# Weight sums by accumulating transfers, a fifth pair of weight buffers and another product order in a seven-product multiplication

## The chip, the cores and the metric

The kernel runs on one core of a Trainium2 chip. TensorE (PE) multiplies, VectorE (DVE) and ScalarE (ACT) do the elementwise work, GpSimd (POOL) does a little of it and issues the transfers that add to their destination, and SyncE (SP) issues most of the others. The metric is the device time of one execution in microseconds (us); lower is better.

## The reference

Two layers act on h, 512 tokens by 2048 channels. Layer 0 holds an attention and a recurrent mixer; the change does not touch it. Layer 1 is a gated unit with a spatial mix, and a second projection that gates a per-layer embedding:

```python
xn = rms_norm(h, norm_pre[1])
u, v, g = split(xn @ c_w_in, (2048, 2048, 2048))
u, v = gelu(u), layer_norm(gelu(v), c_ln_g, c_ln_b)
mixed = einsum('gts,nsgc->ntgc', tril(c_w_s), v in 4 chunks of 128 tokens and 16 groups) + c_b_s
y = ((u * mixed) * silu(g)) @ c_w_out
h = h + rms_norm(y, norm_post[1])
out = h + (p[1] @ ple_w_proj[1]) * sigmoid(h @ ple_w_gate[1])
```

All arrays are float32, and the weights come from HBM.

## The kernel before

**Numbers.** A float32 operand is split in a high part (a cast by ScalarE) and a low part (the rest, a subtraction by VectorE). A product of two operands is three matmuls: high by high, high by low, low by high. The parts of W are made in `pieces`: line 1453 casts, line 1454 subtracts, for one block of 128 rows by 512 columns at a time. They lie in the tiles `whi` and `wlo`, each with four buffers (pool `wsp`).

**Seven products.** The matrices c_w_in (three of 2048 x 2048, for v, u and g), c_w_out and ple_w_gate[1] are multiplied in `seven` (line 1459), in the manner of Strassen and Winograd. W is handled in pairs: a pair covers 1024 columns, as two column halves of 512 and two row halves of 1024. That gives four blocks, W(row half, column half), and seven products take the place of eight. Each product uses one sum of blocks of W and one sum of blocks of the activations, which was prepared before (`sums`). A product has eight steps, one for each 128 rows; a step is six matmuls of 512 columns in line 1489 (twelve of 256 columns in the multiplication by c_w_out).

The W side of the products, per two rows of blocks (128 x 1024 tiles, index j from 0 to 3):

- 1: W(0,0), loaded by SP (line 1401); the tile is kept as `E[j]`
- 5: `E[j]` plus W(0,1), added by an accumulating transfer that POOL issues (`grow`, line 1405)
- 2: W(1,0), loaded
- 6: W(1,1) is loaded and kept as `H[j]`; VectorE adds it to `E[j]` (line 1409)
- 3: `H[j]`, or W(1,1) loaded afresh if `H` is gone
- 7: `H[j]` plus W(0,1), an accumulating transfer
- 4: `E[j]` plus W(1,0), the last block. A pair with `whole` set uses an accumulating transfer of 512 KB. Any other pair loads two halves of 256 KB (line 1446) and VectorE adds each (line 1409). The halves lie in `half0` and `half1`, one buffer each; the very last pair of the kernel has eight slots of its own (`yl8` to `yl15`).

In the kernel before, `whole` is set for both pairs of g and for the first pair of the last matrix. v, u, c_w_out and the second pair of the last matrix load halves.

**Order.** c_w_in goes v, u and g in turn: the two pairs of v interleaved (`FIRST`), then u's first pair, g's first, u's second, g's second, each in the order 1, 2, 5, 6, 3, 4, 7 (`NEXT`). c_w_out and ple_w_gate[1] use `FIRST` too; its last pair ends with 5, 6 and then 3, 4, 7, or what the caller names: 4, 7, 3 in the last matrix. What is done with finished products (lines 1494 to 1538) writes sums to `comb` tiles and emits results: for the last matrix a sigmoid (line 1275), a multiplication with a fetched tile `pj` (1276), an addition (1278) and a store (1280).

**Beside it.** A clock counts steps (`tick`), and `later` hangs other work on it. During u and g that is the mix, 16 groups: a load of v's rows from HBM (`sq` from `vd`, line 1594, issued by ScalarE), four normalizations by ScalarE (1603), POOL masking the mix weights (1606), two VectorE operations (1607, 1608), the split in parts (1613 to 1619), three matmuls (1624 to 1626) and a product into u (1628). The group number e of each half starts 38 + int(7.1 e) steps after u's second product, its load 11 steps sooner, its normalization 4 sooner. In the last matrix `first_fetch` brings `pj` tiles; those of n = 1 lie in `half0` and `half1`.

Each engine's order of instructions is fixed when the program is built: by program order, by priorities (the casts and subtractions of W have a raised one) and by when an operand and a buffer are expected to be there.

Of the kernel before, what the change touches and what calls it, by code (L numbers as in the profile page):

```python
# [9 lines left out]
F32 = mybir.dt.float32  # L10
F32R = mybir.dt.float32r
AF = mybir.ActivationFunctionType
ALU = mybir.AluOpType
# [3 lines left out]
P = 128  # L17
T = 512
# [51 lines left out]
def f(ap):  # L70
# [3 lines left out]
FIRST = lambda a, b, end=(3, 4, 7): [  # L74
    (b, 1, False), (a, 1, True), (b, 2, True), (a, 2, True),
    *[(a, n, True) for n in (5, 6, 3, 4, 7)], *[(b, n, True) for n in (*NEXT[2:4], *end)],
]
# [18 lines left out]
class Pair:  # L96


    def __init__(self, W, c0, n, emit):
        self.W, self.c0, self.n, self.emit = W, c0, n, emit  # L100
        self.whole, self.half = False, None
        self.E, self.H, self.acc, self.R, self.done = {}, {}, {}, {}, set()


class Net:
# [911 lines left out]
    def run(self):  # L1017
        tc = self.tc
        with ExitStack() as ctx:
            pool = lambda name, bufs: ctx.enter_context(tc.tile_pool(name=name, bufs=bufs))  # L1020
            cp, xp = pool("cp", 1), pool("xp", 1)
            self.wraw, self.wsp = pool("wraw", 2), pool("wsp", 4)
            self.xp = xp
            dp = ctx.enter_context(tc.tile_pool(name="dp", bufs=1, space=bass.MemoryType.DRAM))
            self.yd = [self.t(dp, [P, T], f"yd{n}") for n in range(8)]
            self.gd = [self.t(dp, [P, T], f"gd{n}") for n in range(len(AHEAD))]
            self.fd = self.t(dp, [16, T], "fd")
            self.xd = self.t(dp, [P, KT, T], "xd")
            self.hd = self.t(dp, [P, KT, T], "hd")
            self.pd = self.t(dp, [P, 4, D], "pd")  # L1030
            self.vd, self.yd2 = (self.t(dp, [P, c, 4, P], n) for n, c in (("vd", KT), ("yd2", 8)))
            self.homes = {}
            self.clock, self.todo = 0, []
            self.ahead = {}
            self.weng = tc.nc.vector
            self.side, self.beats, self.gate_ins = [], 0, (None, None)
            self.y = [None] * 16
            self.layer_ab(cp, pool)
            self.rest(cp)
# [83 lines left out]
    def last_layer(self, cp, fs, turn, wp, ps):  # L1123
        nc, tc, i = self.nc, self.tc, self.i
# [4 lines left out]
        accq = [self.t(wp, [P, T], "accq", bufs=1), self.rstdB]  # L1129
# [74 lines left out]
        nxt, _, x2, s1, s24, s3, x22 = self.sums(H, wp, SETS)  # L1204
# [36 lines left out]
        def fetch(n, m, o):  # L1241
            pj[n, m] = o
            nc.sync.dma_start(o, self.pd[:, m, n * T : (n + 1) * T])

        def first_fetch(n):
            for m in range(2):
                fetch(n, m, self.t(self.wq, [P, T], f"half{m}") if n == 1 else self.slot("yh", 2 - n + m, F32))

        def next_fetch():
            for j, ns in enumerate(((1, 0), (3, 2))):  # L1250
# [31 lines left out]

        W = i["ple_w_gate"][1]
        pairs = [Pair(W, 2 * j * T, 2 * j, emit) for j in range(2)]
        pairs[0].whole = True
        pairs[1].half = lambda k: self.slot("yl", 8 + k, F32)
        self.seven(FIRST(*pairs, (4, 7, 3)), Sets(nxt), ps)
        self.clock += 100
        self.tick()

# [99 lines left out]
    def pieces(self, pr, prod, keep):  # L1390


        nc = self.nc
        block = lambda kh, ch, j: pr.W[
            (8 * kh + 2 * j) * P : (8 * kh + 2 * j + 2) * P, pr.c0 + ch * T : pr.c0 + ch * T + T
        ].rearrange("(k p) c -> p k c", p=P)
        view = lambda tl: tl.rearrange("p (k c) -> p k c", c=T)

        def load(*where):
            tl = self.piece()  # L1400
            nc.sync.dma_start(view(tl), block(*where))
            return tl

        def grow(tl, *where):
            nc.gpsimd.dma_start(view(tl), block(*where), accum_op=ALU.add)

        def add(tl, other):
            with self.tc.high_priority(self.wpri):
                nc.vector.tensor_tensor(tl, tl, other, ALU.add)

        for j in range(4):
            done = None
            if prod == 1:
                tl = load(0, 0, j)
                if keep:
                    pr.E[j] = tl
                else:
                    done = tl
            elif prod == 5:
                if j not in pr.E:  # L1420
                    pr.E[j] = load(0, 0, j)
                tl = pr.E[j]
                grow(tl, 0, 1, j)
            elif prod == 2:
                tl = done = load(1, 0, j)
            elif prod == 6:
                pr.H[j] = load(1, 1, j)
                tl = pr.E[j]
                add(tl, pr.H[j])
            elif prod == 3:  # L1430
                if j in pr.H:
                    tl = pr.H[j]
                else:
                    tl = done = load(1, 1, j)
            elif prod == 7:
                tl = done = pr.H.pop(j)
                grow(tl, 0, 1, j)
            elif pr.whole:
                tl = done = pr.E.pop(j)
                grow(tl, 1, 0, j)  # L1440
            else:
                tl = done = pr.E.pop(j)
                for a in range(2):
                    g = pr.half(2 * j + a) if pr.half else self.t(self.wq, [P, T], f"half{a}")
                    k = 8 + 2 * j + a
                    nc.sync.dma_start(g, pr.W[k * P : (k + 1) * P, pr.c0 : pr.c0 + T])
                    add(tl[:, a * T : (a + 1) * T], g)
            for a in range(2):
                src = tl[:, a * T : (a + 1) * T]
                hi = self.t(self.wsp, [P, 512], "whi", F32R)  # L1450
                lo = self.t(self.wsp, [P, 512], "wlo", F32R)
                with self.tc.high_priority(self.wpri):
                    self.cast = nc.scalar.copy(hi, src)  # L1453
                    nc.vector.tensor_tensor(lo, src, f(hi), ALU.subtract)  # L1454
                yield 2 * j + a, hi, lo
            if done is not None:
                self.gone(done)

    def seven(self, order, sets, ps, after=lambda n: None, fm=False):


        nc, tc = self.nc, self.tc
        for step, (pr, prod, keep) in enumerate(order):
# [3 lines left out]
            acc = pr.acc[{2: 1, 3: 5}.get(prod, prod)]  # L1467
# [5 lines left out]
            for k, hi, lo in self.pieces(pr, prod, keep):  # L1473
                rows.append((k, hi, lo))
                if k not in hold:
                    for m in range(2):
                        for r, hi, lo in rows:
                            xh, xl = hs[r // 2][:, r % 2, :], ls[r // 2][:, r % 2, :]
                            more = dict(skip_group_check=True)
                            for a in range(2) if fm else (None,):  # L1480
# [7 lines left out]
                                for j, (x, y) in enumerate(parts):  # L1488
                                    nc.tensor.matmul(  # L1489
                                        o, x, y, start=(first and r == 0 and j == 0 and not a), stop=(r == 7 and j == 2), **more  # L1490
# [3 lines left out]
            for m in range(2):  # L1494
                a = acc[m]
# [12 lines left out]
                        nc.vector.scalar_tensor_tensor(a, a, -1.0, pr.R[1][:, m], ALU.mult, ALU.subtract)  # L1508
                        pr.emit(pr, m, pr.n + 1, a)
            pr.done.add(prod)  # L1510
            if prod == 4 and 7 not in pr.done:
                if 3 not in pr.done:
                    for m in range(2):
                        c22, u = pr.R[5][:, m], pr.R[1][:, m]
                        nc.vector.tensor_tensor(c22, c22, u, ALU.add)
                        nc.vector.tensor_tensor(acc[m], acc[m], u, ALU.subtract)
            elif prod == 7 and 3 not in pr.done:
                for m in range(2):
                    c22 = pr.R[5][:, m]
                    nc.vector.tensor_tensor(c22, acc[m], c22, ALU.add)  # L1520
                    pr.emit(pr, 2 + m, pr.n + 1, c22)
                c21 = self.t(self.rp, [P, 2, T], "comb")
                for m in range(2):
                    nc.scalar.copy(c21[:, m], acc[m])
                    nc.vector.tensor_tensor(c21[:, m], pr.acc[4][m], c21[:, m], ALU.subtract)
                    pr.emit(pr, 2 + m, pr.n, c21[:, m])
            elif prod == 7:
                u3 = pr.R[7] = pr.R[1]
                for m in range(2):
                    nc.vector.tensor_tensor(u3[:, m], acc[m], pr.R[1][:, m], ALU.add)  # L1530
                    c22 = pr.R[5][:, m]
                    nc.vector.tensor_tensor(c22, c22, u3[:, m], ALU.add)
                    pr.emit(pr, 2 + m, pr.n + 1, c22)
                if 4 in pr.done:
                    for m in range(2):
                        u = u3[:, m]
                        nc.vector.tensor_tensor(u, pr.acc[4][m], u, ALU.subtract)
                        pr.emit(pr, 2 + m, pr.n, u)
            after(step)

    def add_sq(self, accq, src, n, wp):
# [11 lines left out]
    def layer_c(self, cp, sets, accq, after, wp, ps):  # L1553
# [79 lines left out]
        V = [Pair(W, D + 2 * j * T, 2 * j, vals) for j in range(2)]  # L1633
        U = [Pair(W, 2 * j * T, 2 * j, gates) for j in range(2)]
        G = [Pair(W, 2 * D + 2 * j * T, 2 * j, silu) for j in range(2)]
        for pr in G:
            pr.whole = True
        order = FIRST(*V)
        for pr in (U[0], G[0], U[1], G[1]):
            order += [(pr, prod, True) for prod in NEXT]  # L1640
# [30 lines left out]
        def done(step):  # L1671
# [20 lines left out]
            for j in range(2):  # L1692
                if step == nv + 14 * j + 1:
                    for e in range(8):
                        mix(8 * j + e, 38 + int(7.1 * e))
            if step == nv + 13:
                for n in range(2):
                    self.later(4, lambda n=n: saved(n))
# [290 lines left out]
```

## Time and profile before

| | us |
|---|---|
| three runs, median | 2249.3 |
| lowest and highest | 2247.73, 2253.25 |
| the profiled execution, whole | 2247.82 |
| its span in the profile | 2245.8 |
| granted TensorE clock, mean | 0.997 |
| c_w_in: first product starts at | 1385.9 |
| u's first pair starts at | 1540.0 |
| multiplication by c_w_out starts at | 1882.7 |
| last matrix starts at | 2074.5 |
| last matmul starts at | 2238.5 |

The times come from a profiler record of one execution. Its page gives busy time by engine, a strip of 40 slices, DMA queues, the chain that ended last and the costliest groups of instructions. Further views give who waited for whom, the busy time of chosen stretches, and instructions in order of time. "PE busy" counts each matmul from its start to its modelled end; neighbouring matmuls overlap, so it can show a busy engine while it loses time. In a group, `whi<-rq` means that a tile `whi` was written from a tile `rq`; W's tiles are called `raw` and `rq`, v's rows are `sq`, accumulators in PSUM are `mm`. `yl`, `yh`, `xl` and `xh` are the places of the activations' parts, and a change of name in line 1489 marks the next product or pair of products.

### The profile page before, as it was taken

To read this page: it belongs to the slowest core of one execution; us is meant where nothing else is said; L and a number is where in the kernel's file an instruction comes from. 1 tells how busy PE (TensorE), PEld (TensorE's weight loads), DVE (VectorE), ACT (ScalarE), POOL (GpSimd) and SP (SyncE) were. 2 spreads that over 40 slices of the span, in tenths; PEclk is the share of its full clock that TensorE was granted. 3 is DMA by queue.
4 is the path that set the end of the run, shared out by engine and by line. 5 is a ranking of instruction groups with operands and counts; after the bars stand their busy time and mean duration, and the time that the engine had idled before them with its cause. 6 is when DMAs were issued, how large, how long until landed. Compare 5 with 4: busy or idle time off the path is not lost. (4 is left out here: it accounts for less than half of the span.)

```text
span 2245.8 us, 40515 instructions
## 1 busy us (share of the span) xinstructions
PE 2209.3 (98%) x15369; PEld 1835.5 (82%) x15369; DVE 1543.0 (69%) x3000; ACT 1274.4 (57%) x2599; POOL 260.4 (12%) x316
## 2 busy tenths in 40 slices
PE   8999999999999999999999999999999999999998
PEld 7878888888888788887888888888778778998886
DVE  8766667666734777883227346987677678888968
ACT  5545545555543677773235445756565567657754
POOL 2000010101000000000010011110121121010020
PEclk9999999999999999999999999999999999999999
DMA  7322322223233633334334345687677786488695
GB/s 236 92 79 61 84 76 79 79 66 86 71 89 101 212 93 105 99 104 143 97 103 158 121 123 142 169 212 207 179 171 204 180 193 169 137 210 259 196 247 156
DMA packets 294641, 313.79 MB, mean 140 GB/s; under 512 B 14973, under 2 KB 190750, under 8 KB 293422
## 3 DMA queue, kind: packets, MB, share of 16 engines
q1 hardware_dynamic: 247534, 249.32, 36.1%
q0 software_dynamic: 25024, 48.24, 12.4%
q10 hardware_dynamic: 21888, 13.64, 2.3%
q8 instruction: 121, 1.98, 0.4%
q14 instruction: 74, 0.61, 0.1%
HBM read 280.45 MB, written 30.70 MB: 139 GB/s over the span
## 5 line engine op out<-in xcount | busy, mean ns | idle before, releaser
L197 DVE TENSOR_TENSOR wlo<-raw,whi 128x512 fp32r<-128x512 f32 x400 | 283.4, 717 | 300.6 <-ACT whi L195 265.5
L195 ACT CAST whi<-raw 128x512 fp32r<-128x512 f32 x400 | 247.2, 619 | 345.2 <-PE mm L212 144.1
L212 PE MATMUL mm<-xl,whi 128*128 128x512 f32 x1056 | 414.6, 393 | 0.0
L211 PE MATMUL mm<-xh,whi 128*128 128x512 f32 x992 | 412.0, 415 | 0.0
L213 PE MATMUL mm<-xh,wlo 128*128 128x512 f32 x992 | 391.9, 395 | 0.0
L1454 DVE TENSOR_TENSOR wlo<-rq,whi 128x512 fp32r<-128x512 f32 x432 | 292.3, 685 | 117.1 <-ACT whi L1453 115.8
L1453 ACT CAST whi<-rq 128x512 fp32r<-128x512 f32 x432 | 264.9, 620 | 186.2 <-PE mm L1489 111.8
L212 PEld LDWEIGHTS mm<-xl,whi 128*128 128x128 f32 x1056 | 199.3, 189 | 32.3
L213 PEld LDWEIGHTS mm<-xh,wlo 128*128 128x128 f32 x992 | 186.4, 188 | 41.3
L211 PEld LDWEIGHTS mm<-xh,whi 128*128 128x128 f32 x992 | 187.1, 189 | 33.2
L1489 PE MATMUL mm<-whi,yh 128*128 128x512 f32 x512 | 163.9, 395 | 5.2 <-ACT whi L1453 5.2
L1489 PE MATMUL mm<-whi,yl 128*128 128x512 f32 x512 | 163.7, 393 | 1.1 <-ACT comb L1500 1.1
L1489 PE MATMUL mm<-whi,xl 128*128 128x512 f32 x512 | 163.3, 392 | 0.4 <-ACT whi L1453 0.4
L1489 PEld LDWEIGHTS mm<-whi,yh 128*128 128x128 f32 x512 | 96.9, 189 | 27.1 <-ACT whi L1453 6.9
L1489 PEld LDWEIGHTS mm<-whi,yl 128*128 128x128 f32 x512 | 96.0, 188 | 21.9 <-ACT comb L1500 2.0
L1489 PEld LDWEIGHTS mm<-whi,xl 128*128 128x128 f32 x512 | 96.1, 188 | 21.3 <-ACT whi L1453 0.8
L1454 DVE TENSOR_TENSOR wlo<-raw,whi 128x512 fp32r<-128x512 f32 x128 | 86.9, 686 | 30.6 <-ACT whi L1453 30.2
L1453 ACT CAST whi<-raw 128x512 fp32r<-128x512 f32 x128 | 78.3, 621 | 47.6 <-PE mm L1489 27.4
L1489 PE MATMUL mm<-wlo,yh 128*128 128x512 f32 x256 | 102.0, 398 | 2.0 <-DVE wlo L1454 1.9
L1489 PE MATMUL mm<-wlo,xl 128*128 128x512 f32 x256 | 100.2, 392 | 2.6 <-DVE wlo L1454 2.6
L1489 PE MATMUL mm<-wlo,yl 128*128 128x512 f32 x256 | 100.2, 391 | 1.2 <-DVE wlo L1454 1.1
L1489 PE MATMUL mm<-whi,xh 128*128 128x512 f32 x256 | 80.8, 391 | 0.0
(527 smaller groups left out, 4658.6 us busy)
## 6 DMA issues: line engine op xcount, KB each, us to landing
raw<-in_ab_w_in_dram SPq DMA_DIRECT2D x128, 512.0 KB, 3.9
rq<-in_c_w_in_dram SPq DMA_DIRECT2D x50, 512.0 KB, 4.9
rq<-in_c_w_in_dram POOLq DMA_DIRECT2D x44, 512.0 KB, 7.8
raw<-in_ple_w_gate_dram SPq DMA_DIRECT2D x42, 512.0 KB, 4.2
raw<-in_ab_w_out_dram SPq DMA_DIRECT2D x32, 512.0 KB, 3.8
raw<-in_c_w_in_dram SPq DMA_DIRECT2D x26, 512.0 KB, 5.5
rq<-in_c_w_out_dram SPq DMA_DIRECT2D x24, 512.0 KB, 11.5
rq<-in_ple_w_gate_dram SPq DMA_DIRECT2D x22, 512.0 KB, 4.7
```

Of the source, the lines that this page charges most:

```text
L195: nc.scalar.copy(hi[:, : m * n], src)
L197: self.weng.tensor_tensor(lo[:, : m * n], src, f(hi[:, : m * n]), ALU.subtract)
L211: nc.tensor.matmul(acc, hi, xhi[k], start=(k == 0), stop=False)
L212: nc.tensor.matmul(acc, hi, xlo[k], start=False, stop=False)
L213: nc.tensor.matmul(acc, lo, xhi[k], start=False, stop=(k == nk - 1))
L1453: self.cast = nc.scalar.copy(hi, src)
L1454: nc.vector.tensor_tensor(lo, src, f(hi), ALU.subtract)
L1489: nc.tensor.matmul(o, x, y, start=(first and r == 0 and j == 0 and not a), stop=(r == 7 and j == 2), **more)
```

## The change

1. `whole` becomes the default and v's two pairs alone clear it. u's two pairs, both pairs of c_w_out and the second pair of the last matrix now add product 4's last block by accumulating transfers.
2. Where a pair is `whole`, every fifth pair of high and low parts goes to `half0` and `half1` in place of `wsp`.
3. The second pair of the last matrix ends with products 7, 4, 3 in place of 4, 7, 3. The code for finished products has one form for both orders now: product 7 takes a fresh `comb` tile if product 3 is still to come, and the sum that needs both 4 and 7 is emitted behind whichever is later.
4. The `pj` tiles of n = 1 lie in `accq` and `rstdB`, since the halves are in use.
5. The mix's groups start 40 + int(6.8 e) steps after u's second product.

```diff
@@ Pair
-        self.whole, self.half = False, None
+        self.whole = True
@@ run
+            self.turns = 0
@@ last_layer
         def first_fetch(n):
+            if n == 1:
+                places = self.t(wp, [P, T], "accq", bufs=1), self.rstdB
+            else:
+                places = [self.slot("yh", 2 - n + m, F32) for m in range(2)]
             for m in range(2):
-                fetch(n, m, self.t(self.wq, [P, T], f"half{m}") if n == 1 else self.slot("yh", 2 - n + m, F32))
+                fetch(n, m, places[m])
...
-        pairs[0].whole = True
-        pairs[1].half = lambda k: self.slot("yl", 8 + k, F32)
-        self.seven(FIRST(*pairs, (4, 7, 3)), Sets(nxt), ps)
+        self.seven(FIRST(*pairs, (7, 4, 3)), Sets(nxt), ps)
@@ pieces
-                    g = pr.half(2 * j + a) if pr.half else self.t(self.wq, [P, T], f"half{a}")
+                    g = self.t(self.wq, [P, T], f"half{a}")
...
-                hi = self.t(self.wsp, [P, 512], "whi", F32R)
-                lo = self.t(self.wsp, [P, 512], "wlo", F32R)
+                self.turns = (self.turns + 1) % 5
+                if self.turns or not pr.whole:
+                    hi = self.t(self.wsp, [P, 512], "whi", F32R)
+                    lo = self.t(self.wsp, [P, 512], "wlo", F32R)
+                else:
+                    hi, lo = (self.t(self.wq, [P, T], f"half{x}", F32R) for x in range(2))
@@ seven, behind a product
-            if prod == 4 and 7 not in pr.done:
-                if 3 not in pr.done:
-                    for m in range(2):
-                        c22, u = pr.R[5][:, m], pr.R[1][:, m]
-                        nc.vector.tensor_tensor(c22, c22, u, ALU.add)
-                        nc.vector.tensor_tensor(acc[m], acc[m], u, ALU.subtract)
-            elif prod == 7 and 3 not in pr.done:
-                for m in range(2):
-                    c22 = pr.R[5][:, m]
-                    nc.vector.tensor_tensor(c22, acc[m], c22, ALU.add)
-                    pr.emit(pr, 2 + m, pr.n + 1, c22)
-                c21 = self.t(self.rp, [P, 2, T], "comb")
-                for m in range(2):
-                    nc.scalar.copy(c21[:, m], acc[m])
-                    nc.vector.tensor_tensor(c21[:, m], pr.acc[4][m], c21[:, m], ALU.subtract)
-                    pr.emit(pr, 2 + m, pr.n, c21[:, m])
-            elif prod == 7:
-                u3 = pr.R[7] = pr.R[1]
+            if prod == 7:
+                u3 = pr.R[7] = pr.R[1] if 3 in pr.done else self.t(self.rp, [P, 2, T], "comb")
                 for m in range(2):
                     nc.vector.tensor_tensor(u3[:, m], acc[m], pr.R[1][:, m], ALU.add)
...
-                if 4 in pr.done:
-                    for m in range(2):
-                        u = u3[:, m]
-                        nc.vector.tensor_tensor(u, pr.acc[4][m], u, ALU.subtract)
-                        pr.emit(pr, 2 + m, pr.n, u)
+            if prod in (4, 7) and {4, 7} <= pr.done:
+                for m in range(2):
+                    u = pr.R[7][:, m]
+                    nc.vector.tensor_tensor(u, pr.acc[4][m], u, ALU.subtract)
+                    pr.emit(pr, 2 + m, pr.n, u)
@@ layer_c
-        for pr in G:
-            pr.whole = True
+        for pr in V:
+            pr.whole = False
...
-                        mix(8 * j + e, 38 + int(7.1 * e))
+                        mix(8 * j + e, 40 + int(6.8 * e))
```

## The prediction

> **What bounds the kernel now.** I read the page, then the matrix line's own waits, then a table of stretches, then the rows of the engine that comes last. Times are us; a row of a timeline is start, duration, instruction, and in brackets the idle time before it with what ended it.
>
> ```profile
> span 2245.8 us, 40515 instructions
> PE 2209.3 (98%) x15369; PEld 1835.5 (82%) x15369; DVE 1543.0 (69%) x3000; ACT 1274.4 (57%) x2599; POOL 260.4 (12%) x316
> L1454 DVE TENSOR_TENSOR wlo<-rq,whi 128x512 fp32r<-128x512 f32 x432 | 292.3, 685 | 117.1 <-ACT whi L1453 115.8
> L1453 ACT CAST whi<-rq 128x512 fp32r<-128x512 f32 x432 | 264.9, 620 | 186.2 <-PE mm L1489 111.8
> ```
>
> TensorE bounds it, and no edit removes a matmul. So the change can only win back time in which TensorE waits, and only in the seven-product multiplications. The waits of line 1489 name what it waits for, the two parts of W:
>
> ```profile
>   DVE wlo L1454: 21.4, 40
>   ACT whi L1453: 13.2, 10
> ```
>
> "Busy" overlaps pipelined matmuls, so I count lost time by stretches between product boundaries instead: length, then line 1489's matmuls in it (two belong to the neighbours), then further columns, with the granted clock as the third last.
>
> ```profile
> core 0: us, PE busy (x) PEld busy (x), PEclk, DMA share, GB/s
> 1572.66:1594.42 21.76, 21.76 (x98) 18.02 (x96) 1.00 0.69 158
> 1594.42:1622.38 27.96, 24.95 (x97) 18.77 (x96) 0.94 0.68 210
> 1763.28:1790.21 26.93, 23.51 (x97) 17.63 (x96) 1.00 0.76 206
> 1966.84:1978.36 11.52, 11.52 (x99) 11.52 (x98) 1.00 0.99 261
> 2013.78:2026.75 12.97, 11.99 (x99) 11.62 (x97) 1.00 0.95 211
> 2179.93:2191.49 11.56, 11.46 (x49) 8.86 (x48) 1.00 1.10 270
> 2191.49:2205.29 13.80, 11.46 (x50) 8.77 (x48) 1.00 0.94 229
> ```
>
> The first row is the undisturbed pace: two products, 96 matmuls, 21.76; 10.88 a product, 1.36 for one of its eight steps. The second row is products 4 and 7 of u's first pair: 6.20 over. The third is the same place in u's second pair: 5.17 over. In the output projection a product takes 11.52; the product at 2013.78 takes 12.97, 1.45 over. In the last matrix the product at 2191.49, number 6 of the last pair, is 13.80 − 10.88 = 2.92 over.
>
> What comes last in u and g is ScalarE, which also carries the spatial mix and stands in its queue for v's rows:
>
> ```profile
> ACT sq L1603 <- DMA sq<-vd: 42.7, 16, 5.3
> 1600.58 0.49 ACT L1603 ACTIVATE sq<-sq,nb,rv 128x128 f32<-128x128 f32 x1 [3.54 <-DMA sq<-vd]
> 1612.78 1.26 ACT L1603 ACTIVATE sq<-sq,nb,rv 128x128 f32<-128x128 f32 x3 [5.06 <-DMA sq<-vd]
> 1769.73 0.49 ACT L1603 ACTIVATE sq<-sq,nb,rv 128x128 f32<-128x128 f32 x1 [3.83 <-DMA sq<-vd]
> 1782.14 1.26 ACT L1603 ACTIVATE sq<-sq,nb,rv 128x128 f32<-128x128 f32 x3 [5.26 <-DMA sq<-vd]
> 1836.10 0.49 ACT L1603 ACTIVATE sq<-sq,nb,rv 128x128 f32<-128x128 f32 x1 [3.27 <-DMA sq<-vd]
> 1854.33 0.88 ACT L1603 ACTIVATE sq<-sq,nb,rv 128x128 f32<-128x128 f32 x2 [4.16 <-DMA sq<-vd]
> ```
>
> While ScalarE stands there no part of W is cast. With four buffers the casts are at most four steps ahead, 5.44; the step being read (1.36), a cast (0.62) and a subtraction (0.69) come off: 2.77 of cover. The six waits shown are the ones above it. The other ten share 42.7 − 25.1 = 17.6, 1.8 each.
>
> **The change, part by part.**
>
> *Additions moved to transfers.* Five pairs lose eight loads of 256 KB on SP and eight VectorE additions each, and get four accumulating transfers of 512 KB from POOL.
>
> ```profile
> L1409 DVE TENSOR_TENSOR rq<-rq,half x40: 672/691/694, 1442.1 to 2018.4; 128x512 f32<-128x512 f32 x40
> L1446 SPq DMA_DIRECT2D half<-in_c_w_in_dram x32: 327/328/468, 1225.0 to 1749.9; - x32
> L1446 SPq DMA_DIRECT2D half<-in_c_w_out_dram x16: 327/334/346, 1752.0 to 2013.3; - x16
> L1446 SPq DMA_DIRECT2D yl<-in_ple_w_gate_dram x8: 328/362/412, 2182.6 to 2191.9; - x8
> L1405 POOL DMA_DIRECT2D rq<-in_c_w_in_dram x44: 1188/1203/1707, 1396.7 to 1852.7; - x44
> q1 hardware_dynamic: 247534, 249.32, 36.1%
> q0 software_dynamic: 25024, 48.24, 12.4%
> ```
>
> v keeps 16 of the 32 loads, so 16 + 16 + 8 = 40 go, with 40 additions: 40 x 0.691 = 27.6 of VectorE. Most of that is not on the path, since VectorE is 69% busy; it counts only where a late addition stands before a subtraction. There are two such places:
>
> ```profile
> 2018.35 0.69 DVE L1409 TENSOR_TENSOR rq<-rq,half 128x512 f32<-128x512 f32 x1 [1.38 <-DMA half<-in_c_w_out_dram]
> 2198.50 0.69 DVE L1409 TENSOR_TENSOR rq<-rq,yl 128x512 f32<-128x512 f32 x1 [1.48 <-DMA yl<-in_ple_w_gate_dram]
> 2199.85 0.50 PE L1489 MATMUL mm<-wlo,xl 128*128 128x512 f32 x1 [2.34 <-DVE wlo L1454]
> ```
>
> At both, an addition for product 4 waits for its load, VectorE works its queue in order, and subtractions that TensorE needs stand behind it. With the additions gone I take back all of 1.45 and 2.92. Bounds: nothing, if an accumulating transfer is as late; all, if not. I take all, because ScalarE and VectorE ask for product 4's data only when they cast it.
>
> On SP 40 issues of 0.33 go, and with them the places where the next block's load stood behind a waiting one. On POOL 20 issues of 1.20 come, 24.1, on an engine that is 12% busy. Queued behind them are product 7's transfers and the mix's masking; both are due one product (10.88) or more later, and four issues take 4.8.
>
> All the accumulating transfers are q0: 92 of 0.524 MB are 48.2 MB. They occupy 0.124 x 2245.8 / 92 = 3.03 of all sixteen DMA engines each. A load of 256 KB costs 0.361 x 2245.8 / 249.32 x 0.262 = 0.85. So 20 x 3.03 − 40 x 0.85 = 26.5 more engine time over the 633 from 1572.66 to 2205.29, 4%. On a load of v's rows, which takes about 7.3 to land (its issue near 1593.3, ended at 1600.58), that is 0.3; times the six critical waits, 1.8, less what the fifth buffer hides. I charge 1.5; bounds 0 and 6.
>
> *The fifth buffer.* One step more ahead: cover 2.77 + 1.36 = 4.13. The four u waits exceed 2.77 by 0.77, 2.29, 1.06 and 2.49, 6.61 together, and exceed 4.13 by 0.93 and 1.13, 2.06. Measured loss there is 6.20 + 5.17, of which the slower clock is (1 − 0.94) x 27.96 = 1.7; the remaining 9.7 is 1.46 times my 6.61, because the four normalizations lie between the casts as well. Gain: 1.46 x (6.61 − 2.06) = 6.6. The two in g exceed 2.77 by 0.50 and 1.39 and 4.13 by 0.03: 1.46 x 1.86 = 2.7. And the 1.7 of slow clock, which follows the 2.1 idle here:
>
> ```profile
> 1614.60 0.50 PE L1489 MATMUL mm<-whi,yh 128*128 128x512 f32 x1 [2.10 <-ACT whi L1453]
> 1615.32 0.67 PE L1489 MATMUL mm<-wlo,yh 128*128 128x512 f32 x1 [0.22 <-DVE wlo L1454]
> ```
>
> I take the slow clock as a consequence of this stall, so that it goes with it. [...]
>
> *The moved mix.* Its first steps come two k-steps later and the spacing is 6.8 instead of 7.1. The same instructions; it may move a wait either way by a step, 1.36. I cost it at nothing and keep ±3.
>
> *Order 7, 4, 3 in the last pair.* No instruction more, nearly. Product 7 must now find its data one product earlier. POOL issues the four transfers here:
>
> ```profile
> 2180.55 1.20 POOL L1405 DMA_DIRECT2D raw<-in_ple_w_gate_dram  x1 [4.55 <-DVE rq L1409]
> 2192.45 1.20 POOL L1405 DMA_DIRECT2D rq<-in_ple_w_gate_dram  x1 [1.14 <-ACT whi L1453]
> DMA to landing us min/median/max: 5.8/8.2/15.0
> ```
>
> Product 7 would begin near 2191.49 + 10.88 = 2202.4; its last block is read six steps later, 2210.5, and cast 1.3 before. 2192.45 + 8.2 = 2200.7 is early enough; even 15.0 gives 2207.5. Cost nothing, hidden by product 6; bound 2.
>
> At the end, four emissions no longer fall into product 3, only two. In the old tail the last product's multiplication stood behind another emission's addition:
>
> ```profile
> 2239.84 0.58 ACT L1275 ACTIVATE mm<-mm 128x512 f32<-128x512 f32 x1 [1.36 <-DVE mm L1508]
> 2240.91 0.69 DVE L1276 TENSOR_TENSOR mm<-mm,xh 128x512 f32<-128x512 f32 x1
> ```
>
> The sigmoid ends at 2240.42, the multiplication starts at 2240.91: 0.5 gained.
>
> *Sum.* 6.6 + 2.7 + 1.7 + 1.45 + 2.9 + 0.5 − 1.5 = 14.4. The profiled execution took 2247.8 (2.0 around its span), 1.5 under the median of 2249.3. So 2233.4 for its like, and a median of 2234.9, say 2235.
>
> **The rivals.**
>
> *The fifth buffer buys nothing.* The queues' order is fixed when the program is built, so casts one step further ahead may only bring the normalizations one step nearer to their load, or a step may wait for the halves' own turn. Then only the output projection and the last pair gain: 1.45 + 2.9 + 0.5 − 1.5 = 3.4, some 2246. For it: all sixteen normalizations found ScalarE waiting. Against: TensorE's loss follows the length of the wait.
>
> *More than the sum.* The second wait of each u pair lies behind casts that were late from the first. If the first no longer bites, the 11.4 of u goes whole, and with it some of g: 2.1 x 1.46 = 3.0 and about 4 more, 2228.
>
> *Slower: the heavier transfers delay v's rows.* If every load of v's rows lands d later, six waits lengthen by d against 1.36 of new cover; from d = 1.36 the buffer is used up. At d = 3 the six lose 6 x 1.64 = 9.8 and the other ten, 1.8 + 3 against 4.13, some 6.7: 16.5 lost, 4.9 gained elsewhere, 2249.3 + 12 = 2261. For it: the DMA shares of 0.68 to 1.10 above. Against: the 4%, and g's pairs already accumulate everything. [...]
>
> **How the numbers follow.** Forecast 0.56; no use of the buffer 0.22; more 0.12; slower 0.10. The forecast's own range is 2229 to 2242 by its bounds. 2228 to 2247 takes in the first two rivals and leaves out the slower one and the tails. 0.3% is 6.7 us, about what a measurement here can tell: faster means below 2242.6. Forecast and "more" give 0.68 for faster, the buffer's failure goes to the same, 0.23 with a little else, and slower is 0.09.
>
> **What would show it.** Right: the stretch of u's products 4 and 7 at 24 or less instead of 27.96 and 26.93, with granted clock 1.00; no idle of 2.34 in the last pair's product 6; 16 loads of halves left; the total of ScalarE's waits for v's rows about as now, but TensorE not following. Wrong: TensorE waiting for wlo or whi behind an accumulating transfer; waits for v's rows over 6; new idle at the start of product 7 in the last pair.

## The result, and the profile after

Four runs of the changed kernel gave a median of 2235.36 us (2234.51 to 2237.41); the kernel before, beside them on the same chip, 2248.52 (2245.35 to 2253.25). The ratio is 0.9941, with a 95% interval of 0.9922 to 0.996: faster by 13.2 us, at a forecast of 2235. The total was met, but not by all of its own steps: g lost time where the sum had a gain, v lost some for which it had nothing, and smaller terms gave part of that back.

The page of the changed kernel, whose profiled execution took 2237.41:

```profile
span 2235.7 us, 40381 instructions
PE 2204.7 (99%) x15369; PEld 1832.9 (82%) x15369; DVE 1520.0 (68%) x2958; ACT 1271.6 (57%) x2597; POOL 280.8 (13%) x336
q1 hardware_dynamic: 241774, 238.83, 34.8%
q0 software_dynamic: 30464, 58.73, 15.3%
```

The edit is there: q1 lost 249.32 − 238.83 = 10.5 MB, the 40 half loads, and q0 gained as much, 20 transfers of 0.52 MB. VectorE has 42 instructions and 23 us less. The number of matmuls is the same.

The same stretches between product boundaries as in the prediction, of the changed kernel (the matmul line is 1496 now; the granted clock is the third column from the right): v's last two products, u's products 4 and 7, g's first pair, u's second pair, g's second pair, the output projection's product, and of the last pair product 5, product 6, products 7 and 4, and product 3 with the tail.

```profile
core 0: us, PE busy (x) PEld busy (x), PEclk, DMA share, GB/s
1517.22:1540.44 23.22, 22.30 (x97) 17.94 (x96) 1.00 0.82 238
1594.84:1616.88 22.04, 22.04 (x98) 17.73 (x96) 1.00 0.69 215
1616.88:1707.91 91.03, 82.20 (x338) 61.92 (x337) 1.00 0.78 186
1762.31:1786.57 24.26, 22.40 (x97) 17.71 (x96) 1.00 0.70 195
1786.57:1878.41 91.84, 82.19 (x338) 61.96 (x337) 1.00 0.80 195
2009.45:2020.97 11.52, 11.52 (x99) 11.52 (x97) 1.00 1.12 236
2174.43:2185.41 10.98, 10.98 (x49) 8.93 (x48) 1.00 1.06 221
2185.41:2196.57 11.16, 11.16 (x50) 8.93 (x48) 1.00 1.02 180
2196.57:2218.49 21.92, 21.92 (x98) 17.95 (x96) 1.00 0.84 245
2218.49:2235.70 17.21, 11.04 (x49) 8.82 (x47) 0.96 0.16 61
```

And those of before that the prediction did not show: v's last two, g's two pairs, the last pair's products 4 and 7, and its product 3 with the tail.

```profile
1518.26:1540.02 21.76, 21.76 (x98) 18.02 (x96) 1.00 0.92 268
1622.38:1708.88 86.50, 79.51 (x338) 62.38 (x336) 1.00 0.79 189
1790.21:1882.74 92.53, 83.02 (x338) 61.63 (x337) 1.00 0.80 189
2205.29:2227.86 22.57, 22.42 (x98) 17.78 (x97) 1.00 0.50 152
2227.86:2245.80 17.94, 11.04 (x49) 8.82 (x47) 0.94 0.25 88
```

Set beside each other, row by row, these and the prediction's rows give the account:

| place | forecast | measured |
|---|---|---|
| u's two pairs, with the slow clock | −8.3 | −5.92 − 2.67 = −8.6 |
| g's two pairs | −2.7 | +4.53 − 0.69 = +3.8 |
| v's last two products | 0 | +1.5 |
| output projection's product | −1.45 | −1.45 |
| last pair's product 6 | −2.9 | −2.64 |
| last pair's products 5, and 7 and 4 | 0 | −0.58 − 0.65 = −1.2 |
| last pair's product 3 and tail | −0.5 | −0.73 |
| denser DMA, charged over all | +1.5 | none seen (below) |
| c_w_in begins at 1384.6, not 1385.9 | 0 | −1.3 |

The measured rows make −10.6, the spans −10.1. Both profiled executions lie off their medians (2237.41 is 2.05 above, 2247.82 is 0.7 below), which is the rest of the 13.2: 10.4 + 2.75. c_w_in's start lies ahead of every edit and was anywhere from 1382.3 to 1386.2 in the thirteen profiled executions, so its 1.3 is no gain of the change. A granted clock below 1.00 in a row ahead of the tail is read, here and below, as stretches at half clock of 3.41 us, the length of the one at 1615.48 in the kernel before (last section); by that estimate one of them costs TensorE up to 1.7.

ScalarE's waits for v's rows, in g's first pair and in g's second, before:

```profile
ACT sq L1603 <- DMA sq<-vd: 11.0, 6, 2.6
ACT sq L1603 <- DMA sq<-vd: 13.9, 6, 4.2
```

and after:

```profile
ACT sq L1594 <- DMA sq<-vd: 17.7, 6, 4.8
ACT sq L1594 <- DMA sq<-vd: 14.4, 5, 3.4
```

In g's first pair they rose by 6.7 and the longest from 2.6 to 4.8, and there TensorE lost 4.5. In g's second pair the sum stayed, the longest fell from 4.2 to 3.4, and TensorE gained 0.7. Over u and g together they went from 42.7 to 45.8: the change removed none of this waiting; it altered where TensorE feels it.

The loss in v I had not foreseen. In the changed kernel's timeline of ScalarE stands a cast into the fifth buffer, `half`, ahead of casts that v's last product needs.

```profile
1521.50 0.62 ACT L1460 CAST whi<-rq 128x512 fp32r<-128x512 f32 x1 [0.74 <-PE mm L1496]
1526.32 0.62 ACT L1460 CAST half<-rq 128x512 fp32r<-128x512 f32 x1 [4.19 <-DMA rq<-in_c_w_in_dram]
1526.85 0.61 ACT L1460 CAST whi<-rq 128x512 fp32r<-128x512 f32 x1
```

That cast belongs to u's first pair, eleven casts later. Its buffer was free, since v does not use it, so the fixed order placed it early, and ScalarE stood 4.19 for a block of W that was not due. The casts behind it came late, and v's last two products took 1.46 longer.

### The profile page after: what moved, and what is told of

The parts are those of the page before. It is cut to its first block, busy times and chain, and to the rows that moved or that the text cites. A ratio compares the mean times of both kernels' runs of the same rounds, so it can differ in the third digit from the quotient of the medians.

```text
span 2235.7 us, 40381 instructions
## 1 busy us (share of the span) xinstructions
PE 2204.7 (99%) x15369; PEld 1832.9 (82%) x15369; DVE 1520.0 (68%) x2958; ACT 1271.6 (57%) x2597; POOL 280.8 (13%) x336
## 3 DMA queue, kind: packets, MB, share of 16 engines
q1 hardware_dynamic: 241774, 238.83, 34.8%
## 4 chain that ended last, share of the span: by engine, by line
PE 85%; DMA 5%; DVE 5%; ACT 3%; issue 1%; ACTq 0%; SPq 0%; DVEq 0%
PE mm L1496 28%; PE mm L211 11%; PE mm L213 10%; PE mm L212 10%; PE mm L993 4%; PE mm L994 4%; PE mm L995 4%; DMA sq<-vd 2%; PE tm L549 1%; DMA rq<-in_c_w_in_dram 1%; PE tm L570 1%; DVE wlo L1461 1%; PE g L921 1%; PE pp L338 1%; PE tm L482 1%
## 5 line engine op out<-in xcount | busy, mean ns | idle before, releaser
L1461 DVE TENSOR_TENSOR wlo<-rq,whi 128x512 fp32r<-128x512 f32 x361 | 244.7, 686 | 99.3 <-ACT whi L1460 98.8
L1460 ACT CAST whi<-rq 128x512 fp32r<-128x512 f32 x361 | 221.6, 620 | 141.0 <-PE mm L1496 73.3
L1496 PE MATMUL mm<-whi,yl 128*128 128x512 f32 x440 | 143.6, 393 | 0.4 <-ACT whi L1460 0.2
L1496 PE MATMUL mm<-whi,yh 128*128 128x512 f32 x432 | 138.8, 392 | 2.2 <-ACT whi L1460 2.2
L1496 PE MATMUL mm<-whi,xl 128*128 128x512 f32 x432 | 139.7, 392 | 0.9 <-ACT whi L1460 0.6
L1496 PEld LDWEIGHTS mm<-whi,yh 128*128 128x128 f32 x432 | 81.1, 188 | 19.8 <-ACT whi L1460 3.1
L1496 PEld LDWEIGHTS mm<-whi,xl 128*128 128x128 f32 x432 | 81.1, 188 | 18.5 <-ACT whi L1460 1.0
L1408 POOL DMA_DIRECT2D rq<-in_c_w_in_dram x52 | 62.8, 1207 | 216.5 <-DVE wlo L1461 149.6
L1496 PE MATMUL mm<-wlo,yh 128*128 128x512 f32 x216 | 84.9, 393 | 2.6 <-DVE wlo L1461 2.6
L1496 PE MATMUL mm<-wlo,xl 128*128 128x512 f32 x216 | 84.6, 392 | 0.6 <-DVE wlo L1461 0.5
```

The source lines that it names most:

```text
L1496: nc.tensor.matmul(o, x, y, start=(first and r == 0 and j == 0 and not a), stop=(r == 7 and j == 2), **more)
```

## The experiments

My theory: TensorE's loss in u and g is ScalarE standing for v's rows beyond the cover of the four buffers, a fifth buffer adds one step of cover, and transfers in place of VectorE's additions cure the two places in c_w_out and the last matrix. The rivals: the gain in u comes from the moved mix or from the transfers, not from the buffer; and the last pair gains by the order of its products. Each kernel was timed beside the kernel before on its own chip; ratios are to that.

### Taking the change apart

**Four buffers everywhere**, all else as changed:

```diff
-                if self.turns or not pr.whole:
+                if True:
```

> The changed kernel with four buffers for W's parts everywhere; all else of the change stays. Theory A (the fifth buffer covers ScalarE's waits for v's rows): u's stretch of products 4 and 7 goes back from 22.03 to 26 to 28 in the first pair and from 24.26 to 26 to 27 in the second, the time rises by 7 to 11 us, to 2242 to 2246. Theory B (the gain in u comes from the additions that left VectorE and SP): the stretches stay at 22 and 24, the time within 3 us of 2235. Theory C (the gain in u comes from the mix that starts two steps later): as B.

2238.69 us against 2247.69, ratio 0.9951 (0.9938 to 0.9963): 3.3 above the change by the medians and 2.2 by the ratios, while theory A asked for 7 to 11. v's last two products, u's two stretches, g's first and second pair:

```profile
1514.70:1536.46 21.76, 21.76 (x97) 18.02 (x96) 1.00 0.88 258
1590.86:1615.29 24.43, 22.37 (x97) 17.70 (x96) 1.00 0.65 202
1615.29:1704.65 89.36, 81.34 (x338) 63.43 (x337) 0.98 0.80 189
1759.05:1784.76 25.71, 23.96 (x98) 18.91 (x96) 0.93 0.71 211
1784.76:1878.84 94.08, 83.01 (x337) 61.72 (x337) 1.00 0.78 183
```

u is 50.14, against 46.30 with the buffer and 54.89 before: with the moved mix in place the buffer brings 3.84 in u, 0.6 in g, and costs 1.46 in v. Its net in the kernel as changed is some 3 us, which the intervals of the two ratios do not separate from zero. Up to 3.4 of it is half clock, one stretch in g's first pair (0.98) and one in u's second (0.93), where the changed kernel has none.

**The mix where it was**, all else as changed:

```diff
-                        mix(8 * j + e, 40 + int(6.8 * e))
+                        mix(8 * j + e, 38 + int(7.1 * e))
```

> The changed kernel with the mix's old starting steps, 38 + int(7.1 e). Theory A: u's two stretches within 1.5 us of 22.0 and 24.3, the time within 3 us of 2235. Theory C: u's stretches back to 26 to 28, the time up by 6 to 9 us.

2235.09, ratio 0.9937 (0.9924 to 0.995), the same as the change. u is 24.15 + 22.35 = 46.50; each stretch missed what was expected by about 2, one above and one below. g's two pairs:

```profile
1619.35:1709.02 89.67, 80.78 (x338) 63.09 (x336) 0.98 0.79 188
1785.77:1876.43 90.66, 82.21 (x337) 63.17 (x336) 0.98 0.80 197
```

Together that is 180.3. So the moved mix brings nothing beside the fifth buffer: it gives u 0.2 and takes 2.5 from g. Each pair of g holds one stretch of half clock here (0.98), the changed kernel's none; without them g would take some 177 by my estimate, and the moved mix would cost it up to 6.

**The transfers alone**: four buffers, the mix and the order as before, all else as changed.

```diff
-                if self.turns or not pr.whole:
+                if True:
...
-                        mix(8 * j + e, 40 + int(6.8 * e))
+                        mix(8 * j + e, 38 + int(7.1 * e))
...
-        self.seven(FIRST(*pairs, (7, 4, 3)), Sets(nxt), ps)
+        self.seven(FIRST(*pairs, (4, 7, 3)), Sets(nxt), ps)
```

> The accumulating transfers alone: four buffers, old mix, old order. Theory A: u's stretches as before the change (27 to 28 and 26 to 27), the output projection's product at 11.5 and the last pair's product 6 at 11, so 4 to 6 us are gained on the kernel before: 2243 to 2245. Theory B: 10 us or more are gained, 2239 or less.

2245.36, ratio 0.9985 (0.9974 to 0.9996). u's two stretches, and the last pair's product 6 and products 4 and 7:

```profile
1592.40:1620.14 27.74, 24.73 (x98) 18.72 (x96) 0.94 0.65 202
1762.42:1788.55 26.13, 24.31 (x97) 18.87 (x96) 0.93 0.68 214
2188.33:2200.49 12.16, 11.37 (x50) 8.60 (x48) 1.00 1.06 198
2200.49:2224.46 23.97, 23.18 (x97) 17.90 (x97) 1.00 0.66 190
```

u is 53.87, hardly less than the 54.89 before, and g 87.88 + 92.63 = 180.5 against 179.0. From here the fifth buffer with the old mix (the experiment above) takes u to 46.50: −7.4. But both of u's stretches hold half clock here (0.94 and 0.93), before only the first, and with the buffer neither. With 1.7 taken off for each, an estimate from single executions, u is 53.2 before, 50.5 with the transfers and 46.5 with the buffer: the transfers give u some 2.7, the buffer some 4.0, and the rest is the clock. So the additions and loads that went were not all hidden in u. Together u and g cost 234.4 against 233.9 before, and ScalarE's waits for v's rows were 39.9 in place of 42.7. So neither the contention that I charged with 1.5 nor the rival that feared it is seen in these sums.

In the last pair the transfers alone give product 6 back 1.6 of its 2.9, and products 4 and 7 take 1.4: nothing gained.

**The order 4, 7, 3 again**, all else as changed:

```diff
-        self.seven(FIRST(*pairs, (7, 4, 3)), Sets(nxt), ps)
+        self.seven(FIRST(*pairs, (4, 7, 3)), Sets(nxt), ps)
```

> The changed kernel with the last pair ending 4, 7, 3 again. The prediction's own step: only the tail changes, 0.5 to 1 us behind the last matmul, 2235 to 2237. Rival: the order is what removed the 2.3 us idle in product 6 of the last pair; then it comes back, and the time is 2238 or more.

2244.08, ratio 0.9977 (0.9968 to 0.9987): the order that I priced at nothing. The last pair's product 6, products 4 and 7, and product 3 with the tail:

```profile
2186.67:2199.61 12.94, 11.04 (x50) 8.83 (x48) 1.00 1.06 192
2199.61:2224.57 24.96, 24.34 (x97) 19.18 (x97) 0.93 0.60 175
2224.57:2243.00 18.43, 11.04 (x49) 8.83 (x47) 0.87 0.23 85
```

From product 5 to the end the last pair takes 67.21, in the changed kernel 61.27, before 65.87. Who is late: ScalarE's waits in this kernel from 2175 on, and the first matmul of product 4.

```profile
ACT whi L1460 <- DMA rq<-in_ple_w_gate_dram: 12.1, 5, 2.9
```

```profile
2199.61 0.51 PE L1496 MATMUL mm<-whi,yh 128*128 128x512 f32 x1 [1.90 <-ACT whi L1460]
```

Product 4 follows 6 at once, its accumulating transfers land late, ScalarE stands 12.1 for them (7.5 in the changed kernel, 3.1 of it before a cast into the fifth buffer), and the clock falls to 0.93 behind it. With 7 between 6 and 4 the transfers have a product's time, 10.88, more.

**Half loads and additions in the last pair, with the order 7, 4, 3**:

```diff
...
+        pairs[1].half = lambda k: self.slot("yl", 8 + k, F32)
...
-            elif pr.whole:
+            elif pr.whole and not pr.half:
...
-                    g = self.t(self.wq, [P, T], f"half{a}")
+                    g = pr.half(2 * j + a) if pr.half else self.t(self.wq, [P, T], f"half{a}")
```

> The changed kernel, but the last pair's product 4 loads its eight halves to the old slots and VectorE adds them, as before the change; order 7, 4, 3, fifth buffer and all else as changed. The prediction's step (the additions that left VectorE won the last pair's 4.6): product 6 of the last pair goes back to 13 to 14, 3 to 4 us lost, 2238 to 2240. Theory E (the order won it): from product 5 of the last pair to the end within 1 us of the changed kernel's 61.3, the time within 2 us of 2235.

2241.4 against 2246.92, ratio 0.9975 (0.9965 to 0.9984). Product 6 of the last pair, in one row of the stretches, then VectorE's addition and TensorE's wait:

```profile
2189.92:2205.26 15.34, 12.83 (x50) 10.06 (x48) 0.89 0.78 200
```

```profile
2199.72 0.69 DVE L1413 TENSOR_TENSOR rq<-rq,yl 128x512 f32<-128x512 f32 x1 [1.43 <-DMA yl<-in_ple_w_gate_dram]
2201.07 1.22 PE L1497 MATMUL mm<-half,xl 128*128 128x512 f32 x2 [2.51 <-DVE half L1462]
```

Here is the old kernel's stall again, 15.34 in place of 11.16, up to 1.7 of it half clock behind the stall: the additions for product 4 are what made product 6 late, as I had read it. Products 7 and 4 take 21.77, no loss. So in the last pair the order alone brings 0.6 (65.26 from product 5 on, 65.87 before), or some 2.3 if the half clock is taken off; the transfers alone bring nothing (66.77), both together 4.6. This profiled execution, 2246.04, is the slowest of eleven, the fastest took 2234.44: the rows show the edit at its worst.

### What is left: ScalarE's queue

The waits for v's rows did not go. If they hold TensorE only because casts of W stand behind them, then placing each group's normalizations behind the cast of the step that it belongs to should let them come later, and not wait.

**Normalizations queued behind the step's cast**, all else as changed:

```diff
+                with tc.issue_after(self.cast.ins):
                     for m in range(4):
                         nc.scalar.activation(
...
```

> The changed kernel; the four normalizations of a mix group are queued behind the cast of their own step (seven casts behind the load of v's rows instead of two or three). Theory A (ScalarE standing for v's rows makes the loss that is left in u and g): ScalarE's waits for v's rows fall from about 42 to under 12, u's and g's stretches lose 6 us or more between them, the time is 2230 or less. Rival D (the loss left in g comes from the mix's own chain of VectorE, POOL and matmuls, whenever the rows come): the waits fall, but g keeps its length within 2 us and the time is 2233 to 2238.

2224.92 against 2246.92, ratio 0.99 (0.9886 to 0.9913). ScalarE's waits for v's rows in u and g, and the stretches of u, g, u, g:

```profile
ACT sq L1595 <- DMA sq<-vd: 10.7, 6, 3.6
```

```profile
1598.52:1620.31 21.79, 21.79 (x97) 17.86 (x96) 1.00 0.81 239
1620.31:1703.35 83.04, 78.97 (x337) 62.64 (x337) 1.00 0.83 199
1757.75:1779.54 21.79, 21.79 (x97) 17.85 (x96) 1.00 0.80 239
1779.54:1866.28 86.74, 80.58 (x337) 62.20 (x337) 1.00 0.83 201
```

The waits fell from 45.8 to 10.7, u to 21.79 a stretch where 21.76 is the undisturbed pace, and g by 13.1. So the waits are not owed to the loads' length but to where a normalization stands in the queue. v's last two products took 25.93 here: the cast into the fifth buffer again, for which ScalarE stood 5.55, with half clock behind it (0.93).

**The cast into the fifth buffer queued behind the cast before it**:

```diff
+                    with nullcontext() if self.turns or not pr.whole else self.tc.issue_after(self.cast.ins):
-                    self.cast = nc.scalar.copy(hi, src)
+                        self.cast = nc.scalar.copy(hi, src)
```

> The changed kernel; a cast into the fifth buffer is queued behind the cast of the step before it. Theory F (the fifth buffer, free long before, lets one cast of u's first block be queued ahead of v's last product, where it stands for its load): v's last two products go back from 23.2 to 21.8, 1.5 to 3 us gained, 2232 to 2234. Rival: v's loss stays at 1 us or more, because the load of the block is late in any order.

2234.88, ratio 0.9949 (0.9936 to 0.9961). v's last two products are back at 21.76, so the early cast was the cause there. But the total moved by 0.5 only, and by the ratios not at all, where 1.5 to 3 were expected: u's first stretch went from 22.04 to 23.35, and the waits for v's rows stayed at 44.2.

**All three**: the normalizations behind, the fifth buffer in order, the mix where it was.

```diff
+                    with nullcontext() if self.turns or not pr.whole else self.tc.issue_after(self.cast.ins):
-                    self.cast = nc.scalar.copy(hi, src)
+                        self.cast = nc.scalar.copy(hi, src)
...
+                with tc.issue_after(self.cast.ins):
                     for m in range(4):
                         nc.scalar.activation(
...
-                        mix(8 * j + e, 40 + int(6.8 * e))
+                        mix(8 * j + e, 38 + int(7.1 * e))
```

> The changed kernel with all three: normalizations behind their own step's cast, the fifth buffer's casts in order, and the mix's old starting steps. If theories A and F both hold, the gains add: 2224 to 2229. If D holds, 2231 to 2234.

2221.19, ratio 0.9888 (0.9875 to 0.9902), the fastest of all, 14 us below the change by the medians and some 12 by the ratios. Waits for v's rows, and TensorE from 1540 to 1885, u and g:

```profile
ACT sq L1596 <- DMA sq<-vd: 1.5, 2, 0.8
```

```profile
1540.00:1885.00 345.00, 345.00 (x1635) 288.30 (x1634) 268.06 (x418) 232.01 (x422) 73.09 (x66) 1.00 0.81 193
```

The busy view shows no idle of TensorE left in u and g, 345.00 of 345.00; u takes 21.88 in each stretch, v's last two products 21.76.

**The normalizations behind, alone, on the kernel before**:

```diff
+                with tc.issue_after(self.cast.ins):
                     for m in range(4):
                         nc.scalar.activation(
```

> The kernel before the change with one edit: a mix group's normalizations are queued behind the cast of their own step. Theory A: u's stretches of products 4 and 7 fall from 27.97 and 26.93 to under 23, g loses 6 us or more as well, 14 to 18 us are gained: 2229 to 2233; the last pair and the output projection keep their 4.6 and 1.45 of loss. Rival: with four buffers other waits take the place of v's rows, and less than 8 us are gained, over 2239.

2229.43 against 2248.07, ratio 0.9919 (0.9905 to 0.9933). This one edit gains 18.6, more than the whole change; u goes from 54.89 to 43.79 with four buffers.

**The fastest kernel with four buffers**, to see what the fifth is then still worth:

```diff
-                if self.turns or not pr.whole:
+                if True:
...
-                    with nullcontext() if self.turns or not pr.whole else self.tc.issue_after(self.cast.ins):
-                        self.cast = nc.scalar.copy(hi, src)
+                    self.cast = nc.scalar.copy(hi, src)
```

> The transfers, order 7, 4, 3 and the mix's old starting steps with the normalizations behind their own step's cast, and four buffers: the version with all three edits less the fifth buffer. Theory A (the fifth buffer is worth only the cover of those waits, and they are gone): within 3 us of that version's 2221.2. Rival (the buffer covers other late data too, such as transfers): 2225 or more.

2224.86, ratio 0.9898 (0.9884 to 0.9912), 3.7 above the one with five by the medians and 2.2 by the ratios, whose intervals overlap: the times alone do not show that the fifth buffer is of use here. The profiles differ in two places. In g's second pair ScalarE still waits once for v's rows, for 3.92, where the longest wait with five is 0.8, and the pair takes 89.00 in place of 86.65. The other place has nothing to do with v's rows. One row each of this kernel: ScalarE, TensorE, and the stretch of two products of u's second pair in which they lie, 25.61 in place of 21.76, up to 1.7 of it half clock.

```profile
1722.14 1.28 ACT L1567 ACT_TABLE_LOAD   x1 [3.71 <-DMA yd<-xh]
```

```profile
1724.68 0.50 PE L1496 MATMUL mm<-whi,yl 128*128 128x512 f32 x1 [1.47 <-ACT whi L1460]
```

```profile
1708.09:1733.70 25.61, 23.91 (x97) 19.09 (x96) 0.93 0.45 131
```

u's gelu, with its table load ahead, waits 3.71 for a store out of the tile that it will write, the casts wait behind it, and four buffers do not bridge that. With five, in order, the same stretch is 21.76; there the gelu found its store finished, so how much of the 3.85 is cover and how much another placing in the queue stays open.

**The fastest kernel with the order 4, 7, 3**:

```diff
-        self.seven(FIRST(*pairs, (7, 4, 3)), Sets(nxt), ps)
+        self.seven(FIRST(*pairs, (4, 7, 3)), Sets(nxt), ps)
```

> The version with all three edits, but the last pair ends 4, 7, 3. Theory G (with transfers, product 4 directly behind product 6 finds its data late, whatever went before): from product 5 of the last pair to the end 66 to 68 instead of 61 to 62, 5 to 7 us lost, 2226 to 2229. Rival (the loss under the old order was a matter of that schedule alone): within 2 us of 2221.2.

2226.99, ratio 0.9911 (0.9897 to 0.9925): 5.8 lost by the medians, 5.2 by the ratios, and in the same place: 68.1 from product 5 to the end against 61.9.

## Why the prediction was right, and where not

- **Casts' cover in u: right in kind and in sum, the buffer's share too large.** Forecast −8.3 with the clock, measured −8.6, and −7.4 when only the buffer and the order are added to the transfers. With half clock taken off, some 4.0 of it is the buffer's, which had 6.6 in the sum, and some 2.7 the transfers', which had nothing in u; that the two make up for each other is luck. The wait at 1600 to 1614 no longer stops TensorE, and the clock's 1.7 went with the stall (1.00 in u's first stretch, 0.94 before). In the kernel before, the 3.41 us ahead of the half clock held 2.32 of idle (last section). What I did not see is that with four buffers the moved mix takes u from 53.87 to 50.14, so its gain and the buffer's are not to be added.
- **g: wrong, −2.7 became +3.8.** The step "exceed 2.77 by 0.50 and 1.39 and 4.13 by 0.03" took the waits of the old record as given, and asked only how much cover is set against them. But where the normalizations stand in ScalarE's queue changed with the edits: in g's first pair, where no wait had been above 2.77, the longest grew from 2.6 to 4.8. The step that failed by most is the moved mix, "I cost it at nothing". With the old steps g was 180.3, up to 3.4 of it half clock, beside 180.5 with the transfers alone, so there the buffer may have given the 2.7 that I asked of it; with the moved steps g was 182.9 without any half clock. My rival sentence, that casts further ahead bring the normalizations nearer to their load, held in g only beside the moved mix: there the buffer raised ScalarE's waits for v's rows from 27.4 to 32.1, with the old mix it lowered them from 24.8 to 22.4.
- **v: left out.** I looked for the buffer's effect only where it is used. It also freed an instruction to go early into a queue across a boundary; 1.5, and 4.2 in the kernel with the normalizations moved (25.93), up to 1.7 of that half clock.
- **The moved mix at nothing: right in the medians** (2235.09 without it), not in the rows: it gave u 0.2 and took 2.5 from g, and the half clock in the old mix's g hides part of that loss.
- **Output projection, 1.45: right to the hundredth.** 12.97 became 11.52, also with the transfers alone.
- **Product 6 of the last pair, 2.9: right in size, wrong in whose it is.** The failing steps are "ScalarE and VectorE ask for product 4's data only when they cast it" (true, but in the old order they cast it at once behind product 6) and "Order 7, 4, 3 … Cost nothing". The trace of before had the sign: the half loads themselves arrived 1.48 late there; for the accumulating transfers in their place, in the old order, ScalarE stood 12.1. The order gives the transfers one product's time.
- **Contention, 1.5: not seen**, and with it the rival on the slower side. With the added load the waits for v's rows were 39.9 (the transfers alone), against 42.7 before.
- **The tail, 0.5: 0.73.**

In sum: the terms for u, the output projection, product 6 and the tail were 13.15, and 13.4 was measured. g and v cost 5.3 where the sum had 2.7 of gain, 8.0 missed. The contention that did not come and the last pair's other products gave 2.7 back. That leaves 9.3; c_w_in's earlier start and the spread of single executions around their medians make it 13.2. That 2235.0 was met to 0.4 is in part chance.

What I passed over is larger than all of it. The view of waits showed 42.7 of ScalarE waiting, I quoted the row, and went on to ask how to cover those waits. Asking why a normalization stood at the head of a queue before its load had landed would have led to the 18.6.

## What to carry to other kernels

When an engine waits for a transfer and others need what stands behind the waiting instruction in its queue, first ask whether that instruction can stand further back: in the kernel before that alone took ScalarE's waits for v's rows from 42.7 to 6.4 and gained 18.6 us. One more buffer only lengthened the time that one could stand there (u from 50.14 to 46.30 in the changed kernel), and, being free, let yet another instruction come too early (4.19 of waiting in v). Price edits of one place together when one makes data later and the other asks for it later: here the transfers were worth nothing alone, the order 0.6 us (some 2.3 with half clock taken off), and both together 4.6.

## What the runs showed of the hardware

In the trace of the kernel before the granted clock is 0.50 from 21.46 to 24.88, from 164.82 to 168.24, from 1615.48 to 1618.90, 3.41 us each, and from 2243.54 to the end; everywhere else it is 1.00. In that of the changed kernel it is 0.50 from 2234.48 to the end alone, behind the last matmul. A value such as 0.94 for a row of 27.96 us is the mean over one such stretch; of the other kernels' rows, 0.93 over 25.61 and 0.80 over 8.48 (1723.20 to 1731.68, four buffers with the normalizations behind) come to 1.8 and 1.7 lost, about the one such stretch that both hold. The clock fell behind some stalls of TensorE and not behind others, and the length of the stall does not tell which: it did behind 2.10 in the kernel before and behind the 1.47 shown above, and did not behind 2.34 (shown with the prediction) and 2.26 (1783.96) in the kernel before.

In the kernel before, the four starts are 42, 425 and 184 times 3.413 apart. Stretches of 3.41 cut at whole multiples of this from 1615.48 hold the stall of 2.10 and a gap of 0.22 in one, and the stall of 2.34 in two, 1.65 and 0.69. The columns are PE, PEld, DVE, ACT, POOL, the clock, DMA share and GB/s:

```profile
1612.07:1615.48 3.41, 1.09 (x4) 0.35 (x4) 0.90 (x2) 2.70 (x7) 0.00 (x0) 1.00 0.48 183
1615.48:1618.90 3.42, 3.42 (x9) 2.65 (x10) 3.31 (x6) 1.63 (x3) 0.00 (x0) 0.50 0.35 90
2195.75:2199.16 3.41, 1.76 (x7) 1.05 (x6) 1.40 (x4) 1.24 (x2) 0.00 (x0) 1.00 1.10 258
2199.16:2202.58 3.42, 2.73 (x12) 2.27 (x13) 3.04 (x6) 0.62 (x1) 0.00 (x0) 1.00 1.10 260
```

Idle in such a stretch did not decide alone either: in the same trace half clock followed 1.33 (18.05 to 21.46) and 1.18 (161.41 to 164.82), ahead of c_w_in, and did not follow the 1.65 above. What decides it was not shown. The row from 1615.48 counts 9 matmuls, the 3.40 us behind it 17. Half of 3.41 is the 1.7 us that I take for one such stretch, an estimate; by it the stall of 1.47 cost more than twice its length. So two rows are best compared with their clocks beside them.
